# One PSUM tile per bank for Strassen's down products, and the attention's value projection placed ahead of the rotations

## The chip, the core and the metric

The kernel runs on one core of a Trainium2 chip. Its metric is the device time of one execution in microseconds (us). It is stated as the median of several executions; the profile is a further execution of the same program, recorded by the hardware profiler.

TensorE (PE in the profile, its weight loads PEld) does the matrix products into PSUM, an accumulation memory of eight banks. VectorE (DVE), ScalarE (ACT) and GpSimd (POOL) read PSUM or SBUF and do the elementwise work; SP here only issues DMAs.

## The reference

One step of a two-layer streaming encoder for 512 prompt tokens and 64 tokens of a running stream, 576 in all, at width 1024. Cut to what matters:

```python
for i in range(2):
    h = rmsnorm(x, norm_mix[i])
    y = pool_mixer(h) if i == 0 else attn_mixer(h)
    x = x + y
    u = relu(rmsnorm(x, norm_mlp[i]) @ w_up[i])       # 1024 -> 4096
    x = x + (u * u) @ w_down[i]                       # 4096 -> 1024
y = rmsnorm(x, norm_final)

# attn_mixer: p = h @ w_in is cut into q (16 heads of 64), k and v (4 heads), qi (8 index heads),
# ki (1 index key) and wi (8 weights); q, k, qi, ki are rotated by position
score = sum_h relu(qi_h . ki / 8) * wi_h              # masked by chunk
idx = top_k(score)                                    # up to 256 keys for each query
o = softmax(q . k[idx] / 8) @ v[idx];  y = o @ w_o
```

Keys, values and index keys of the step are outputs as well.

## The kernel before, in words

All matrices lie transposed: features on the 128 partitions, the 576 tokens along the free axis, in two halves of 288 (`HT`). Each fp32 operand is split into a high and a low part, so that one product takes three matmuls (high by high, high by low, low by high). A block of weights, 128 output columns of a matrix, is loaded as one tile by a DMA on ACT's queue, cast by ACT (L166: `wh`) and completed by a subtraction on DVE (L167: `wl`). `jobs` lists these blocks in the order of their use; `next_unit` and `next_block` take from it and keep a few units ready ahead.

The program is written as if it ran in sequence. A scheduler (`schedule_with_timeline_sim`, L1214) then decides the order of the instructions on each engine; only the pool mixer and the tail `last()` have parts ordered by hand. Each engine runs its queue in the built order.

The stages follow each other at L1126 to L1133: the pool mixer, the first MLP, the attention, the second MLP with the tail.

**MLP.** `split_x` scales and splits the residual into `xs` and adds up its squares on the way (L251, L252). Eight up blocks (`project`, L226, 48 matmuls each) make one c, a quarter of the hidden width. The norm's statistics come behind the first ups: `stats` sums the squares over partitions on PE (`st`, L284), a chain of small DVE operations makes the reciprocal root, `spread` puts it on all partitions by two matmuls with a diagonal (`rb`, L264) and ACT copies it to SBUF (L265). Only then can `activated` evacuate an up tile (DVE, L327, the tile times `rb`, cut at zero; ACT squares it). So the up tiles made before that stay in PSUM.

The down product of a c is done by Strassen's scheme (in the first MLP for all four c, in the second for three): `factors` (L335) makes seven right factors from the activations; the weights' sums are made on POOL. `Pair` (L359) handles two output blocks with three accumulators a, b and c. `opening` (L368) runs three products of 12 matmuls, `opened` (L376) lets DVE, and at the last c POOL, read them; `closing` (L391) runs four more products into a, b, c and b, each read by one DVE addition (L396). `down` (L398) goes over four pairs.

**PSUM.** Two pools serve the whole kernel: `ps`, three tiles of two banks, and `po`, two tiles of one bank (L54, L55, handed out by `psum`, L91, and `psum1`, L94). In a `Pair` a and b are the halves of one `ps` tile and c is a `po` tile. The ups take `ps` tiles, `st` and `rb` take `po` tiles. A tile of a pool with n buffers waits for the readers of the n-th tile before it.

**Attention.** `ki` and the first index query block `pj` are projected (48 matmuls each), then the norm is spread, the tables cs and sn are multiplied by it, and `ki` is rotated (L782 to L785). `rope` projects two blocks and rotates them; the two index query halves go first (on DVE, L814 to L827), through DRAM, and come back by the loads into `qis`. Behind them stands the value projection (L1077 to L1095): two blocks `w_v` of 264 columns, the tokens in five groups in the order 1, 2, 3, 4, 0; each has 24 matmuls into half a `ps` tile, one ACT copy to `V` and one DVE operation for `wi`. Into its last group four index scores are mixed. Then come the key rotation, four query rotations, and the units of attention: `scores`, `softmax` (DVE L910, ACT L911), `transpose` (PE L952, `pt`), `values`. `pace` mixes index scores (`ix`, L864 and L879; read by ACT L872 or L874; added up on DVE L882 and L884) into these rotations' projections. `top_k(i)` runs 16 or 18 rounds of a maximum (L895) and a replacement (L896) on DVE and makes the mask (L899); its place in the program is ahead of the first scores of query block i.

The second MLP's first up follows the output projection `wo`, whose tiles DVE adds to the residual (L1123).

Of the kernel before, what the change touches and what calls it, by code (L numbers as in the profile page):

```python
# [24 lines left out]
NIDX = 8  # L25
# [18 lines left out]
def pool_dsa_kernel(ctx: ExitStack, tc: tile.TileContext, a, o):  # L44
    nc = tc.nc
    act, dve, pool, pe = nc.scalar, nc.vector, nc.gpsimd, nc.tensor
# [4 lines left out]
    raws = ctx.enter_context(tc.tile_pool(name="raws", bufs=2))  # L51
    norms = ctx.enter_context(tc.tile_pool(name="norms", bufs=1))
    tiny = ctx.enter_context(tc.tile_pool(name="tiny", bufs=4))
    ps = ctx.enter_context(tc.tile_pool(name="ps", bufs=3, space=PSUM))  # L54
    po = ctx.enter_context(tc.tile_pool(name="po", bufs=2, space=PSUM))  # L55
    dram = ctx.enter_context(tc.tile_pool(name="dram", bufs=1, space=bass.MemoryType.DRAM))

    count = [0]
# [1 line left out]
    def uid(s):  # L60
        count[0] += 1
        return f"{s}_{count[0]}"

    phase = {}

    @contextmanager
    def stage(**pools):

        with ExitStack() as st:
            phase.clear()  # L70
            for name, bufs in pools.items():
                phase[name] = st.enter_context(tc.tile_pool(name=uid(name), bufs=bufs, reuse_waits="tile"))
            yield

    def slot(tag, s, dt=F32R):
# [4 lines left out]
    def pair_slot(tag, s, dt=F32R, n=T):  # L80
        return slot(tag, s, dt)[:, :2 * n].rearrange("p (h t) -> p h t", h=2)
# [6 lines left out]
    def small(n, s):  # L88
        return tiny.tile([P, n], F32, tag=s, name=uid(s))

    def psum(s="ps"):  # L91
        return ps.tile([P, 2, 512], F32, tag="ps", name=uid(s))

    def psum1(s="po"):  # L94
        return po.tile([P, 512], F32, tag="po", name=uid(s))

    def f32(t):
        return t.bitcast(F32)
# [4 lines left out]
    def const(shape, name, dt=F32, pool=None):  # L103
        return (pool or cst).tile(shape, dt, tag=name, bufs=1, name=name)
# [35 lines left out]

    mlp_jobs(0, 4)
    jobs.extend(("block", a["w_in"][j], KT * P) for j in range(5))
    jobs.extend(("block", a["w_v"][j], 4 * 264) for j in range(2))
    jobs.extend(("block", a["w_in"][j], KT * P) for j in range(5, 15))
    for _ in range(2):
        jobs.extend(("block", a["w_o"][m], KT * P) for m in range(KT))
    mlp_jobs(1, 3)
# [78 lines left out]
    def project(pt, w, xs, between=iter(()), cols=((0, HT), (HT, HT))):  # L226

        n = len(xs)
        for k in range(n):
            next(between, None)  # L230
            wh, wl = at(w, k)
            for i, (wt, part) in enumerate(((wh, 0), (wh, 1), (wl, 0))):
                for h, (c, m) in enumerate(cols):
                    pe.matmul(  # L234
                        pt[:, h, :m], wt, xs[k][:, part, c:c + m],
                        start=(k == 0 and i == 0), stop=(k == n - 1 and i == 2),
                    )

    class Norm:
# [14 lines left out]
        def stats(self):  # L254
            pt = psum1("st")
            token_sums(pt, self.s2)
            self.r = rms(pt)

        def spread(self):
            diag = diagonals(self.r)  # L260
            self.rb = tmp("rb" + self.s, "rb", 1)
            for h in range(2):
                pb = psum1("rb")
                pe.matmul(pb[:, :HT], ones, diag[:, h * HT:(h + 1) * HT], start=True, stop=True)  # L264
                act.copy(self.rb[:, h * HT:(h + 1) * HT], pb[:, :HT])  # L265
            return self.rb
# [44 lines left out]
    def split_x(gi, norm, tags, add=dve):  # L311
        xs = []
        for k in range(KT):
            t = pair_slot(tags[k], "xs")
            split(t, x[k], gv[:, gi, k:k + 1])
            norm.add(k, add if k < 6 else dve)
            xs.append(t)
        return xs

    def mlp(layer, gi, strassen, add=dve, end=None):  # L320
        norm = Norm(f"m{layer}")
        xs = split_x(gi, norm, ["xs"] * KT, add)
# [36 lines left out]
        class Pair:  # L359


            def __init__(self, c, q, us):
                self.c, self.q, self.us = c, q, us
                ab = psum("ab")
                self.a, self.b, self.c_ = ab[:, 0], ab[:, 1], psum1("c")
                self.lo, self.hi = ([x[2 * q + i][:, c0:c0 + HT] for i in range(2)] for c0 in (HT, 0))

            def opening(self, parts=((0, 1, 2, 3),)):  # L368
# [36 lines left out]
        v = None  # L405
# [350 lines left out]
    def attention():  # L756
        nonlocal x
        norm = Norm("a")
        xs = split_x(2, norm, ["xs"] * KT)
# [7 lines left out]
        V = const([P, 9, 256], "V", pool=cst)  # L767
        wi = const([P, 5, 8], "wi", pool=cst)
# [6 lines left out]
        r = norm.r  # L775
        p0 = psum("pj")
        project(p0, next_block(), xs)
        rb = norm.spread()
        pool.tensor_tensor(cs, cs, rb, ALU.mult)
        dve.tensor_tensor(sn, sn, rb, ALU.mult)  # L780
        t1, t2, ki = tmp("t1"), tmp("t2"), tmp("ki")
# [281 lines left out]

        def pace():

            due = 0
            for k in range(10 * KT):
                while due <= k and done[0] < 3 * NIDX:
                    next(index)
                    due += PACE[min(done[0] // NIDX, 2)]  # L1070
                    done[0] += 1
                yield

        done = [0]
        index = (None for i in range(1, 5) for _ in index_scores(i))

        wv = [next_block(), next_block()]  # L1077
        for i in (1, 2, 3, 4, 0):
            n = P if i < 4 else TS
            pt = psum("v")[:, 0]  # L1080
            for k in range(KT):
                if i == 0 and k % 2:
                    next(index, None)
                    done[0] += 1
                wh, wl = wv[k // 4][k % 4 // 2]
                sl = slice((k % 2) * 264, (k % 2 + 1) * 264)
                for j, (part, wt) in enumerate(((0, wh), (1, wh), (0, wl))):
                    pe.matmul(pt[:n, :264], xs[k][:, part, i * P:i * P + n], wt[:, sl],  # L1088
                              start=(k == 0 and j == 0), stop=(k == KT - 1 and j == 2))
            vi = i if i < 4 else 8  # L1090
            act.activation(V[:n, vi], pt[:n, :256], AF.Copy, scale=r[:n, i:i + 1])
            dve.tensor_scalar(wi[:n, i], pt[:n, 256:264], r[:n, i:i + 1], NIDX ** -0.5, ALU.mult, ALU.mult)
        act.activation(small(8, "e1"), wi[:, 0], AF.Exp)
        nc.sync.dma_start(o["v_p"], V[:, 0:4])
        nc.sync.dma_start(o["v_s"], V[:TS, 8])  # L1095

        between = pace()
        qd, ks = {}, []
        (k1, k2), st = rope(False)
        nc.sync.dma_start(o["k"][0], k1)  # L1100
        nc.sync.dma_start(o["k"][1], k2)
        for g in range(NKV):
            t = pair_slot("x", "k")
# [16 lines left out]
        for m in range(KT):  # L1120
            pt = psum("wo")
# [1 line left out]
            dve.tensor_tensor(x[m][:, 2 * P:], x[m][:, 2 * P:], pt[:, 0, :T - 2 * P], ALU.add)  # L1123
# [106 lines left out]
```

## Time and profile before

| | |
|---|---|
| three executions | 1164.63, 1165.96, 1166.82 us |
| median | 1165.96 us |
| profiled execution, its own time | 1169.65 us |
| span of its instructions | 1167.8 us |
| instructions | 20621 |
| PE busy | 95% of the span |
| DVE busy | 70% |
| ACT busy | 45% |
| POOL busy | 30% |
| granted PE clock, mean | 0.98 |
| DMA moved | 116.68 MB |

The profiled execution's time is 1.85 us longer than its span, and 3.69 us above the median of the three. Times in the trace are counted from the start of the span. In a row of the timeline the first two numbers are start and length, both in us; "xN" joins N instructions of one kind; in brackets stands how long the engine sat idle just before, and which instruction released it. In a row of waits the numbers are the sum in us, how many times, and the longest. In a row of a group stand the busy time, the mean length of one in ns, and the idle time ahead of it. A row of stretches gives the busy time of PE, PEld, DVE, ACT and POOL with the number of instructions, and then the granted clock of PE as a share of full speed.

### The profile page before, as it was taken

How to read it: one execution, taken by the hardware profiler on the slowest of the kernel's cores; microseconds unless marked ns; L12 is line 12 of the kernel's file. 1: busy time of each engine (PE TensorE's matmuls, PEld its weight loads, DVE VectorE, ACT ScalarE, POOL GpSimd, SP SyncE). 2: the span in 40 equal slices, each digit the busy share in tenths (PEclk: the TensorE clock that was granted, in tenths of full speed). 3: DMA queues.
4: the chain of work that ended last, by engine and by line, in shares of the span. 5: the costliest groups of instructions: out<-in, count | busy, mean ns of one | idle time of the engine just before them, and what ended most of it. 6: DMA issues, size and time to landing. Idle time of an engine off the chain costs nothing.

```text
span 1167.8 us, 20621 instructions
## 1 busy us (share of the span) xinstructions
PE 1110.5 (95%) x8244; PEld 1090.6 (93%) x8244; DVE 817.0 (70%) x1478; ACT 528.9 (45%) x968; POOL 349.9 (30%) x274
## 2 busy tenths in 40 slices
PE   7999999999999999798989999999999999989995
PEld 6999999999999999797979999999999989989995
DVE  7776666767667786759999853876766767775434
ACT  5644344335334444253368665654344335333331
POOL 7711410330240351117775341101410330350002
PEclk8999999999999999798989999999999999999998
DMA  5421241232232134366652432431241132114212
GB/s 172 114 75 52 73 145 55 75 125 73 73 108 91 38 113 161 101 197 158 170 154 74 121 104 81 157 109 55 73 145 55 57 125 90 55 55 122 77 37 82
DMA packets 51152, 116.68 MB, mean 100 GB/s; under 512 B 9345, under 2 KB 22960, under 8 KB 51056
## 3 DMA queue, kind: packets, MB, share of 16 engines
q10 hardware_dynamic: 23184, 84.45, 23.1%
q1 hardware_dynamic: 27872, 30.90, 9.2%
q8 instruction: 65, 1.06, 0.4%
q14 instruction: 31, 0.25, 0.1%
HBM read 99.73 MB, written 13.25 MB: 97 GB/s over the span
## 4 chain that ended last, share of the span: by engine, by line
PE 60%; DVE 15%; issue 12%; POOL 5%; DMA 4%; ACT 3%; SPq 0%; DVEq 0%; ACTq 0%; POOLq 0%
PE up L234 30%; PE ab L356 8%; DVE wl L167 5%; PE dn L234 4%; PE pj L234 4%; PE c L356 3%; DVE work L896 2%; PE o L971 2%; DMA raw<-in_w_up 2%; PE wa L234 1%; DMA pair<-in_w_down 1%; DVE m L895 1%; POOL sum L194 1%; PE v L1088 1%; PE pb L720 1%
## 5 line engine op out<-in xcount | busy, mean ns | idle before, releaser
L234 PE MATMUL up<-xs,wh 128*128 128x288 f32 x2048 | 355.9, 295 | 1.5 <-DVE v L327 1.3
L234 PEld LDWEIGHTS up<-xs,wh 128*128 128x128 f32 x2048 | 299.8, 188 | 2.5 <-DVE v L327 1.7
L356 PE MATMUL ab<-u,wh 128*128 128x288 f32 x1120 | 227.2, 297 | 11.4 <-DVE x L396 5.8
L166 ACT CAST wh<-raw 128x512 fp32r<-128x512 f32 (+1 forms) x210 | 126.0, 619 | 206.2 <-DMA raw<-in_w_up 61.9
L234 PE MATMUL up<-xs,wl 128*128 128x288 f32 x1024 | 219.4, 295 | 0.0
L167 DVE TENSOR_TENSOR wl<-raw,wh 128x512 fp32r<-128x512 f32 (+1 forms) x186 | 144.3, 784 | 70.7 <-ACT wh L166 68.9
L356 PEld LDWEIGHTS ab<-u,wh 128*128 128x128 f32 x1120 | 179.4, 189 | 15.3 <-DVE x L396 8.6
L356 PE MATMUL ab<-u,wl 128*128 128x288 f32 x560 | 165.5, 298 | 2.0 <-DVE wl L167 1.9
L234 PEld LDWEIGHTS up<-xs,wl 128*128 128x128 f32 x1024 | 164.2, 188 | 0.0
L167 DVE TENSOR_TENSOR wl<-pair,wh 128x512 fp32r<-128x512 f32 x112 | 101.4, 917 | 30.5 <-ACT wh L166 30.0
L194 POOL TENSOR_TENSOR sum<-sum,pair 128x512 f32<-128x512 f32 x28 | 41.2, 1472 | 265.4 <-DVE wl L167 265.4
L186 POOL TENSOR_TENSOR sum<-pair 128x512 f32<-128x512 f32 x28 | 38.0, 1357 | 266.7 <-DMA pair<-in_w_down 266.7
L166 ACT CAST wh<-sum 128x512 fp32r<-128x512 f32 x84 | 51.0, 621 | 145.8 <-POOL sum L187 47.7
L356 PEld LDWEIGHTS ab<-u,wl 128*128 128x128 f32 x560 | 105.4, 189 | 3.9 <-DVE wl L167 3.5
L166 ACT CAST wh<-pair 128x512 fp32r<-128x512 f32 x112 | 68.2, 620 | 86.4 <-PE up L234 40.7
L356 PE MATMUL c<-u,wh 128*128 128x288 f32 x448 | 92.5, 295 | 0.4 <-ACT wh L166 0.4
L167 DVE TENSOR_TENSOR wl<-sum,wh 128x512 fp32r<-128x512 f32 x84 | 71.2, 858 | 26.2 <-ACT wh L166 25.4
L327 DVE SCALAR_TENSOR_TENSOR v<-up,rbm 128x576 f32<-128x576 f32 x64 | 48.2, 755 | 58.6 <-PE up L234 57.2
L234 PE MATMUL pj<-xs,wh 128*128 128x288 f32 x448 | 83.5, 304 | 4.1 <-DVE t L783 4.1
L234 PEld LDWEIGHTS pj<-xs,wh 128*128 128x128 f32 x448 | 70.1, 197 | 5.8 <-DVE t L783 4.9
L356 PEld LDWEIGHTS c<-u,wh 128*128 128x128 f32 x448 | 72.4, 189 | 0.7 <-ACT wh L166 0.7
L356 PE MATMUL c<-u,wl 128*128 128x288 f32 x224 | 66.0, 296 | 0.0
(224 smaller groups left out, 1974.6 us busy)
## 6 DMA issues: line engine op xcount, KB each, us to landing
raw<-in_w_up ACTq DMA_DIRECT2D x64, 512.0 KB, 3.6
pair<-in_w_down ACTq DMA_DIRECT2D x56, 512.0 KB, 3.6
raw<-in_w_o ACTq DMA_DIRECT2D x16, 512.0 KB, 4.1
raw<-in_w_in ACTq DMA_DIRECT2D x15, 512.0 KB, 4.0
q<-st SPq DMA_DIRECT2D x32, 144.0 KB, 2.6
q<-q SPq DMA_DIRECT2D x16, 256.0 KB, 3.0
raw<-in_w_down ACTq DMA_DIRECT2D x8, 512.0 KB, 3.5
x<-in_x SPq DMA_DIRECT2D x8, 288.0 KB, 6.3
```

The lines of the kernel that those rows point to most:

```text
L166: act.copy(h, src)
L167: how["sub"].tensor_tensor(l, src, f32(h), ALU.subtract)
L186: pool.tensor_tensor(s1, a21, a22, ALU.add)
L194: pool.tensor_tensor(s2, s2, a12, ALU.add)
L234: pe.matmul(pt[:, h, :m], wt, xs[k][:, part, c:c + m], start=(k == 0 and i == 0), stop=(k == n - 1 and i == 2),)
L327: dve.scalar_tensor_tensor(v, pt[:, :, :HT], 0.0, halves(norm.rb), ALU.max, ALU.mult)
L356: pe.matmul(bank[:, :HT], wt, ut, start=first and j == 0 and i == 0, stop=last and j == 3 and i == 2, skip_group_check=True)
L720: pe.matmul(pt[:, c0:c0 + rhs.shape[1]], lhs, rhs, start=n == 0, stop=n == len(steps) - 1)
L895: dve.max(m8[:np_], wk[:np_])
L896: dve.match_replace(wk[:np_], m8[:np_], wk[:np_], TAKEN)
L971: pe.matmul(oc[:, 2 * s + hh], pT[:, c:c + P], V[:, kt, vs], start=kt == 0, stop=kt == i)
L1088: pe.matmul(pt[:n, :264], xs[k][:, part, i * P:i * P + n], wt[:, sl], start=(k == 0 and j == 0), stop=(k == KT - 1 and j == 2))
```

## The change

The pools `ps` and `po` are no longer made once for the whole kernel but anew in each of the four stages. The pool mixer and the attention get three tiles of two banks and two of one bank as before; both MLPs get **two** tiles of two banks and **four** of one bank. The pools wait for a reuse tile by tile (`reuse_waits="tile"`, which the other stage pools had already). A `Pair` takes three tiles of one bank.

In the attention the value projection goes to just behind `norm.spread()`, ahead of the multiplication of cs and sn. Its groups now come in the order 0 to 4, without index scores among them, and into one-bank `po` tiles. Its two output DMAs move with it, and so stand on SP ahead of the index queries' stores and loads. In `jobs` the two `w_v` blocks come behind two `w_in` blocks instead of five. `pace` begins with index scores after `KT` = 8 steps instead of at once.

```diff
-    ps = ctx.enter_context(tc.tile_pool(name="ps", bufs=3, space=PSUM))
-    po = ctx.enter_context(tc.tile_pool(name="po", bufs=2, space=PSUM))
...
             for name, bufs in pools.items():
-                phase[name] = st.enter_context(tc.tile_pool(name=uid(name), bufs=bufs, reuse_waits="tile"))
+                space = {"space": PSUM} if name in ("ps", "po") else {}
+                phase[name] = st.enter_context(tc.tile_pool(name=uid(name), bufs=bufs, reuse_waits="tile", **space))
...
-    jobs.extend(("block", a["w_in"][j], KT * P) for j in range(5))
+    jobs.extend(("block", a["w_in"][j], KT * P) for j in range(2))
     jobs.extend(("block", a["w_v"][j], 4 * 264) for j in range(2))
-    jobs.extend(("block", a["w_in"][j], KT * P) for j in range(5, 15))
+    jobs.extend(("block", a["w_in"][j], KT * P) for j in range(2, 15))
...
-                ab = psum("ab")
-                self.a, self.b, self.c_ = ab[:, 0], ab[:, 1], psum1("c")
+                self.a, self.b, self.c_ = (psum1(t) for t in "abc")
...
         rb = norm.spread()
+
+        wv = [next_block(), next_block()]
+        for i in range(5):
+            n = P if i < 4 else TS
+            pt = psum1("v")
+            for k in range(KT):
...
+                    pe.matmul(pt[:n, :264], xs[k][:, part, i * P:i * P + n], wt[:, sl],
+                              start=(k == 0 and j == 0), stop=(k == KT - 1 and j == 2))
+            vi = i if i < 4 else 8
+            act.activation(V[:n, vi], pt[:n, :256], AF.Copy, scale=r[:n, i:i + 1])
+            dve.tensor_scalar(wi[:n, i], pt[:n, 256:264], r[:n, i:i + 1], NIDX ** -0.5, ALU.mult, ALU.mult)
+        nc.sync.dma_start(o["v_p"], V[:, 0:4])
+        nc.sync.dma_start(o["v_s"], V[:TS, 8])
         pool.tensor_tensor(cs, cs, rb, ALU.mult)
...
         def pace():
 
-            due = 0
+            due = KT
...
-        wv = [next_block(), next_block()]
-        for i in (1, 2, 3, 4, 0):
-            n = P if i < 4 else TS
-            pt = psum("v")[:, 0]
-            for k in range(KT):
-                if i == 0 and k % 2:
-                    next(index, None)
-                    done[0] += 1
...
         act.activation(small(8, "e1"), wi[:, 0], AF.Exp)
-        nc.sync.dma_start(o["v_p"], V[:, 0:4])
-        nc.sync.dma_start(o["v_s"], V[:TS, 8])
...
-    with stage(slots=1, xs=1, tmps=6):
+    with stage(slots=1, xs=1, tmps=6, ps=3, po=2):
         pool_mixer()
-    with stage(u=1, xs=1, acts=1, tmps=3, pairs=1, more=2):
+    with stage(u=1, xs=1, acts=1, tmps=3, pairs=1, more=2, ps=2, po=4):
         mlp(0, 1, 4, pool)
-    with stage(slots=1, xs=1, cst2=1, tmps=6):
+    with stage(slots=1, xs=1, cst2=1, tmps=6, ps=3, po=2):
         attention()
-    with stage(xs=1, u=1, acts=1, tmps=3, pairs=1, more=2):
+    with stage(xs=1, u=1, acts=1, tmps=3, pairs=1, more=2, ps=2, po=4):
         mlp(1, 3, 3, end=last)
```

More of the change, by code (lines that the diff above doesn't have):

```diff
@@ L91, in psum @@
     def psum(s="ps"):
-        return ps.tile([P, 2, 512], F32, tag="ps", name=uid(s))
+        return phase["ps"].tile([P, 2, 512], F32, tag="ps", name=uid(s))
     def psum1(s="po"):
-        return po.tile([P, 512], F32, tag="po", name=uid(s))
+        return phase["po"].tile([P, 512], F32, tag="po", name=uid(s))
     def f32(t):
@@ L778, in attention @@
         rb = norm.spread()
+        wv = [next_block(), next_block()]
[3 more added lines that the diff above has]
+            for k in range(KT):
+                wh, wl = wv[k // 4][k % 4 // 2]
+                sl = slice((k % 2) * 264, (k % 2 + 1) * 264)
+                for j, (part, wt) in enumerate(((0, wh), (1, wh), (0, wl))):
+                    pe.matmul(pt[:n, :264], xs[k][:, part, i * P:i * P + n], wt[:, sl],
[5 more added lines that the diff above has]
+        nc.sync.dma_start(o["v_s"], V[:TS, 8])
         pool.tensor_tensor(cs, cs, rb, ALU.mult)
@@ L1075, in attention @@
         index = (None for i in range(1, 5) for _ in index_scores(i))
-        wv = [next_block(), next_block()]
-        for i in (1, 2, 3, 4, 0):
-            n = P if i < 4 else TS
-            pt = psum("v")[:, 0]
-            for k in range(KT):
-                if i == 0 and k % 2:
-                    next(index, None)
-                    done[0] += 1
[L1085 to L1092, printed above, removed]
         act.activation(small(8, "e1"), wi[:, 0], AF.Exp)
-        nc.sync.dma_start(o["v_p"], V[:, 0:4])
-        nc.sync.dma_start(o["v_s"], V[:TS, 8])
         between = pace()
```

## The prediction, made before the changed kernel ran

> **What bounds the kernel now.** I read the page's busy times and slices first, then PE's waits, then the timeline where a wait is long or where the change acts, and last the stretches with their clock.
>
> ```profile
> PE 1110.5 (95%) x8244; PEld 1090.6 (93%) x8244; DVE 817.0 (70%) x1478; ACT 528.9 (45%) x968; POOL 349.9 (30%) x274
> ...
> PE   7999999999999999798989999999999999989995
> ...
> PEclk8999999999999999798989999999999999999998
> ...
> L356 PE MATMUL ab<-u,wh 128*128 128x288 f32 x1120 | 227.2, 297 | 11.4 <-DVE x L396 5.8
> ```
>
> PE is the bound: 1110.5 of 1167.8 us, and no slice but those about the attention's start, and the first and the last, is clearly below 9 tenths. The change adds no matmul, so it can win only from the 57.3 us in which PE is idle and from stretches at a low clock. Its waits say whose the idle time is:
>
> ```profile
> PE ab L356 <- DVE x L396: 5.8, 11, 1.3
> PE pt L952 <- ACT p L911: 5.2, 2, 5.1
> PE ix L864 <- ACT rl L872: 5.2, 1, 5.2
> PE pj L234 <- DVE t L783: 4.1, 1, 4.1
> ...
> PE ab L356 <- ACT wh L166: 2.9, 2, 1.5
> ```
>
> The first row is the stall that the product banks are about: 11 times the products waited for DVE to read an accumulator. The fourth is the one that the moved values could fill. The second and third stand further on in the attention; DVE is behind both, as shown below.
>
> **Starts of the MLPs: two up tiles instead of three.** Here the change adds a wait. Before, three ups run before `rb` exists; with `ps` at two, the third up's first matmul waits for DVE's L327 of the first up, and so for the whole norm chain.
>
> ```profile
> 48.39 0.77 PE L234 MATMUL up<-xs,wh 128*128 128x288 f32 x4
> ...
> 61.80 0.76 DVE L252 TENSOR_TENSOR s<-s,sq 128x576 f32<-128x576 f32 x1 [1.32 <-POOL s L252]
> ...
> 63.08 0.75 DVE L252 TENSOR_TENSOR s<-s,sq 128x576 f32<-128x576 f32 x1
> ...
> 65.84 1.16 PE L284 MATMUL st<-ones,s 128*128 128x2 f32 x10
> ...
> 69.17 1.24 PE L264 MATMUL rb<-diag,ones 128*128 128x288 f32 x4 [0.25 <-DVE diag L274]
> ...
> 71.69 0.79 PE L234 MATMUL up<-xs,wh 128*128 128x288 f32 x4 [1.29 <-DVE v L327]
> ```
>
> The order of before puts 131 up matmuls between 48.39 and `st` at 65.84: 0.133 us each, 6.3 us for an up of 48. In the first MLP after, PE's order is up, up, st, rb, rb, up. The two ups end at about 62; `st` needs the last sum of squares. The POOL sum ends at 61.80, and the two DVE additions now stand back to back: 61.8 + 0.76 + 0.75 = 63.3. From `st` to `rb` I take 69.17 - 65.84 = 3.33, and from `rb` to the next up that waits for L327 71.69 - 69.17 = 2.52. The third up starts at 63.3 + 3.33 + 2.52 = 69.2 and ends at 75.4; before, three ups were done at 71.69: **+3.7 us**. (The first up now also waits for the pool mixer's last evacuation, about 1 us; that is inside the wait for 63.3 and costs nothing.) PE runs in order, so the other five ups of this c and all products queue behind the waiting one, and DVE's and ACT's work on them with it; nothing later gives the time back, since PE is the bound.
>
> ```profile
> 750.82 0.70 PE L234 MATMUL up<-xs,wh 128*128 128x288 f32 x4
> ...
> 753.82 0.48 DVE L1123 TENSOR_TENSOR x<-x,wo 128x320 f32<-128x320 f32 x1
> ...
> 758.68 1.15 PE L284 MATMUL st<-ones,s 128*128 128x2 f32 x10
> ...
> 765.80 1.21 PE L264 MATMUL rb<-diag,ones 128*128 128x288 f32 x4 [0.52 <-DVE diag L274]
> ...
> 766.64 0.90 PE L234 MATMUL up<-xs,wh 128*128 128x288 f32 x4
> ...
> 767.48 1.42 DVE L327 SCALAR_TENSOR_TENSOR v<-up,rbm 128x576 f32<-128x576 f32 x2 [0.46 <-ACT rbm L265]
> ```
>
> In the second MLP the stage's new pool makes the first up wait for the last L1123, which ends at 753.82 + 0.48 = 754.3, where before PE went on at 750.82: 3.5 us idle. Then up, st, up: 754.3 + 6.3 + 1.15 + 6.3 = 768.1, `rb`, and the third up again waits for the first L327: `rb` to its end was 767.48 + 0.7 - 765.80 = 2.4, so 770.5 instead of 766.64: **+3.9 us**. Bounds of each: nothing (if the chain is as quick as PE) and 6.3 (one whole up without cover).
>
> To that comes the clock:
>
> ```profile
> 401.00:405.00 4.00, 3.35 (x14) 3.35 (x15) 3.73 (x6) 2.84 (x5) 1.12 (x1) 0.58 0.01 2
> 468.00:478.00 10.00, 3.70 (x15) 2.48 (x15) 4.12 (x12) 1.20 (x4) 1.97 (x1) 0.59 0.18 55
> ...
> 548.00:555.00 7.00, 5.29 (x20) 5.01 (x20) 7.00 (x16) 3.43 (x7) 1.51 (x2) 0.53 0.62 154
> ```
>
> After a break PE comes back at about half clock: 0.42 of 4 us, 1.7 us, in the first row; 0.47 of 7 us, 3.3 us, in the last. The new breaks, some 4.5 of 7 us idle at the first start and 3.5 us in one piece at the second, resemble these rows. I take the middle, 2.6 us each, **+5.2** for both, with bounds of 0 and 3.3 each. The Trainium skill's page "TensorE: Matmul & The Clock Gate", in "HAM oscillation — how this bites in real kernels", asks only that no idle gap exceed about 3.4 us; by that the first start, whose pieces are 1 to 2 us, would keep its clock, and the sum would be 2.6 us lower. The trace speaks against it: its first row stands behind a gap of about 2 us.
>
> **Down stages: four single banks.** Seven stages of four pairs. DVE's reads of a, b and c now release three tiles separately, and the next pair opens in whatever bank came free; the order of after puts about 24 matmuls, 3.2 us, between a read and the product that needs its bank, against waits of at most 1.3 us. The whole gain to be had is the row of 5.8 us. Some reads stay queued behind a weight subtraction on DVE, so I take 60%: **-3.5 us**. Bounds: -5.8, and +5.8 if single banks wait as often again, since c now shares its four banks with a and b.
>
> **Entry to the attention.** Before, 57 matmuls of `ki` and `pj` lay among the last products; after, all products come first and then three projections, 19 us of cover while the residual's splits and squares run. The work is the same; what can go is part of the wait before `st`.
>
> ```profile
> 468.01 1.26 PE L284 MATMUL st<-ones,s 128*128 128x2 f32 x10 [2.28 <-DVE s L252]
> 471.45 2.29 PE L264 MATMUL rb<-diag,ones 128*128 128x288 f32 x4 [2.17 <-DVE diag L274]
> 477.84 1.33 PE L234 MATMUL pj<-xs,wh 128*128 128x288 f32 x4 [4.11 <-DVE t L783]
> ```
>
> The 2.28 us go, the 2.17 us stay: **-2.5 us** with a little from the products. Bounds -5 (these two with part of the last c's waits) and +4 (the projections no longer fill the products' waits, up to the fourth row's size).
>
> **The moved values.** What moves is 120 matmuls, five ACT copies, five small DVE operations and two DMAs; nothing is added. The values' groups now start right behind `rb` and fill the 4.11 us. The two output DMAs go ahead of the index queries' on SP, but `V` is ready about 15 us behind `rb` and those loads were due 21 us behind it: no cost; without that cover, the issue of two DMAs. `pace` and the five groups put the first index score about 3 us later behind `rb`; four more weight subtractions are done by then on DVE, which evens it out. So PE gains 4 to 7 us here, but what comes next is DVE:
>
> ```profile
> 516.00:550.00 34.00, 28.82 (x205) 28.13 (x204) 33.15 (x68) 13.47 (x28) 23.25 (x14) 0.98 0.55 141
> 550.00:594.00 44.00, 38.93 (x272) 38.32 (x271) 43.17 (x92) 16.64 (x32) 31.67 (x21) 0.93 0.59 163
> 594.00:640.00 46.00, 44.77 (x346) 42.42 (x346) 42.96 (x166) 40.15 (x133) 28.73 (x23) 0.94 0.41 109
> 640.00:740.00 100.00, 99.31 (x786) 95.74 (x786) 64.75 (x168) 60.67 (x142) 33.49 (x29) 1.00 0.36 109
> ```
>
> DVE is busy 33.15 of 34 and 43.17 of 44 us: from 516 to 594 it sets the pace, PE's two 5 us waits lie there, and PE wins only if DVE's order changes. It does:
>
> ```profile
> L895 DVE MAX8 m<-work 128x8 f32<-128x256 f32 (+2 forms) x40 | 20.9, 528 | 0.6
> L896 DVE MATCH_REPLACE8 work<-m,work 128x256 f32<-128x256 f32 (+2 forms) x39 | 19.9, 510 | 0.0
> ```
>
> ```profile
> 584.95 0.92 DVE L899 TENSOR_SCALAR work<-work 128x384 f32<-128x384 f32 x1
> ...
> 588.42 0.69 DVE L895 MAX8 m<-work 128x8 f32<-128x512 f32 x1
> ...
> 589.94 0.69 DVE L895 MAX8 m<-work 128x8 f32<-128x512 f32 x1
> ...
> 592.86 0.28 DVE L910 CUSTOM_DVE_ANT_0 p<-sc,mask 128x128 f32<-128x128 f32 x1
> ```
>
> In DVE's order after, the first softmax (592.86 here) has 15 fewer operations ahead of it: five rounds of top_k(3) at 589.94 - 588.42 = 1.52, two of top_k(2) at 0.528 + 0.510 = 1.04, one L899 of 0.92: 7.6 + 2.1 + 0.9 = 10.6 us. These rounds aren't saved, they come later between the units of attention, where the third row still has DVE at 42.96 of 46 us. By the order, about 7 to 8 us are still owed when DVE gets slack (64.75 of 100 us from 640 on). So I take **-7.5 us**. Bounds: -10.6, and +3 (all rounds paid back, index scores 3 us later).
>
> **Sum.** 3.7 + 3.9 + 5.2 - 3.5 - 2.5 - 7.5 = -0.7 us. The tail and the pool mixer keep their order and count as nothing; PE covers what is left there. 1169.65 - 0.7 = 1168.95 us as a profiled execution; that one stood 3.69 us over the median, so 1165.3 us.
>
> **Rivals.**
>
> *DVE takes the attention's gain back* (slower). The deferred rounds fall due before the masks of blocks 2 and 3, and DVE has only 3 of 46 us free there; if it stays above 95% busy until about 640, softmax is as late as before and -7.5 becomes 0: 1165.3 + 7.5 = 1172.8. For it: the third row; against it: PE's wait of 5.1 us on the first softmax would still move.
>
> *Starts at full clock, gains whole* (faster). The half clock doesn't strike (-5.2), the banks take all of 5.8 (-2.3) and the attention all of 10.6 (-3.1): 1165.3 - 10.6 = 1154.7. For it: full clock before through a 1.29 us gap at 71.69; against it: the row at 401.
>
> *The banks don't do what they are for.* The waits on DVE are really waits on weights, as the row of 2.9 us with ACT's cast hints, and only change their name: -3.5 becomes 0, 1168.8.
>
> *Single banks put the down stages at half clock* (slower). The accumulator waits become more frequent, and one row like that at 401 in each of seven stages costs 7 x 1.7 = 12 us: 1177. The slices show full clock through all down stages with their 11 waits, which speaks against it. The same page's "A second HAM failure mode: psum-queue depth-cycling" reports such an oscillation where results cycle through banks; no run here shows it.
>
> **How the numbers follow.** Below 0.2%, 2.3 us, a measurement of this kernel can't be told from no change. Forecast 0.35, with its own range of 1160 to 1171: faster 0.12, same 0.15, slower 0.08. DVE takes it back: 0.30, slower. Full gains: 0.22, faster. Banks without effect: 0.08, same 0.02, slower 0.06. Half clock in the down stages: 0.05, slower. Together faster 0.34, same 0.17, slower 0.49: the likeliest single case is no change, with more ways to lose than to win. The range goes from 1154.5, the full gains, to 1177, the unknown costs' ends without their sums.
>
> **What the profile after would show.** Right: a PE wait of 3.5 us on L1123 at the second MLP's start and about 4.5 us about `st`, `rb` and the third up at the first; the granted clock under 0.7 there; "ab" or a, b, c waits on L396 under 2.5 us in all; no wait on L783; the first `pt` some 10 us earlier behind `rb`. Wrong: waits on L396 as large as before, or PE idle on softmax between 594 and 640 by several us more; or a second MLP that starts without a wait.

## The result, and the profile after

The changed kernel took 1181.59 us (median of 4 executions, 1176.38 to 1183.02), the kernel before 1166.39 (median of 4): a ratio of 1.0116, 95% interval 1.0073 to 1.0158. It is slower, by some 15 us, outside the predicted range; the forecast was no change. The profiled execution has a span of 1181.3 us against 1167.8, 13.5 us more.

The page of the changed kernel:

```profile
PE 1117.8 (95%) x8244; PEld 1096.1 (93%) x8244; DVE 811.7 (69%) x1478; ACT 529.9 (45%) x968; POOL 354.4 (30%) x274
...
PE   7989989999999999999979999899999999999995
...
PEclk8989999999999999999989999999999999999998
...
L356 PE MATMUL b<-u,wh 128*128 128x288 f32 x672 | 139.1, 300 | 10.2 <-DVE x L395 8.1
```

The instructions of PE are as many as before. PE's idle time grew from 57.3 to 63.5 us, and its busy time by 7.3 with the same instructions, so matmuls ran longer: a new dip stands in the third slice of both rows, at the first MLP's start. The last line is the surprise: the single bank b alone waits 8.1 us for the residual's additions, more than a and b together did before. PE's waits:

```profile
PE b L356 <- DVE x L395: 8.1, 8, 2.2
PE pt L967 <- ACT p L926: 7.8, 4, 6.5
...
PE up L234 <- DVE x L1118: 3.4, 1, 3.4
...
PE up L234 <- DVE v L327: 2.7, 2, 1.4
PE ix L879 <- ACT rl L887: 2.7, 1, 2.7
PE c L356 <- DVE x L395: 2.4, 3, 1.2
...
PE ix L879 <- DMA qi<-qi: 1.7, 1, 1.7
```

(L395 and L1118 are the lines 396 and 1123 of before; in the runs below the same additions stand at L394 to L397 and L1118 to L1121.) To place the 13.5 us, I took from each trace the start of the same PE instructions: the first up of each later c, the last `wo` matmul and the first `dn`, a matmul of the down products of the second MLP's last c, which are not by Strassen's scheme. Each column below is how much longer (+) or shorter than in before a stretch was, in us, from those starts; the first stretch starts with the span. PE takes the first up of the next c ahead of a c's down products, so the second row ends ahead of those of c = 2.

| stretch, by its end | before's end | after | banks only | values only | pools per stage | t3 first | subtractions on POOL |
|---|---|---|---|---|---|---|---|
| first MLP, first eight ups | 103.54 | +7.3 | +6.2 | 0.0 | +0.2 | +4.8 | +5.7 |
| its down stages of c = 0 and 1, with the next ups | 297.76 (first up of c = 3) | +7.7 | +6.4 | +0.2 | -0.1 | -0.7 | +1.3 |
| its down stages of c = 2 and 3, and the attention | 750.68 (last wo) | -5.3 | -0.2 | -5.6 | -6.3 | -4.7 | -3.2 |
| second MLP, first eight ups | 804.98 | +5.6 | +5.7 | +0.6 | +2.1 | +5.4 | +5.6 |
| its Strassen stages | 1101.34 (first dn) | -2.4 | -2.8 | -0.2 | 0.0 | -2.2 | -4.6 |
| tail | 1167.8 | +0.6 | +0.5 | +0.5 | +0.4 | +0.5 | +0.6 |

The five kernels on the right are the experiments below. One execution scatters by some 3 us, as the runs of before show (1164.6 to 1171.3), so a difference of 1 us in this table isn't to be read. "The first MLP's down stages" means the second row below.

The third row adds up three things. Two more cuts, at the first product of c = 3 (394.41 in before) and at the end of the spread `rb` (473.73), split it into the stage of c = 2, the stage of c = 3 with the entry to the attention, and the attention from the spread on: +1.1, -1.2 and -5.3 in the changed kernel, +2.0, +0.5 and -2.7 with the banks only, 0.0, -1.6 and -4.0 with the values only.

**The starts.** PE's timeline and its stretches at the first MLP:

```profile
62.99 1.16 PE L284 MATMUL st<-ones,s 128*128 128x2 f32 x10
66.31 2.29 PE L264 MATMUL rb<-diag,ones 128*128 128x288 f32 x4 [2.17 <-DVE diag L274]
69.97 1.30 PE L234 MATMUL up<-xs,wh 128*128 128x288 f32 x4 [1.37 <-DVE v L327]
```

```profile
64.00:72.00 8.00, 4.46 (x14) 3.29 (x14) 4.58 (x15) 3.31 (x7) 0.00 (x0) 0.61 0.19 66
72.00:80.00 8.00, 8.00 (x48) 8.00 (x48) 4.15 (x7) 2.55 (x4) 0.00 (x0) 0.75 0.00 0
```

The third up starts at 69.97 (forecast 69.2) and runs with the clock granted at 0.61 and then 0.75 of full speed: 0.25 of the second stretch is 2 us, and some of the first. The norm chain is the predicted one, st to rb 3.3 us, rb to up 3.7 instead of 2.5, and `rb` itself takes 2.29 us instead of 1.24. At the second MLP:

```profile
763.45 0.48 DVE L1118 TENSOR_TENSOR x<-x,wo 128x320 f32<-128x320 f32 x1
764.08 0.76 PE L234 MATMUL up<-xs,wh 128*128 128x288 f32 x4 [3.40 <-DVE x L1118]
...
782.09 0.77 PE L234 MATMUL up<-xs,wh 128*128 128x288 f32 x4 [1.37 <-DVE v L327]
```

Its 3.40 us on the last L1118 is the wait that was forecast as 3.5, and the third up waits for L327 as forecast. The stretch behind the first wait has its clock at 0.79, so 0.21 of 8 us, 1.7 us, where 2.6 was forecast:

```profile
764.00:772.00 8.00, 7.92 (x48) 7.95 (x49) 4.59 (x7) 3.54 (x6) 0.00 (x0) 0.79 0.47 140
```

**The down stages.** This is the end of the first stage, DVE's and ACT's rows with the product that waits, in the changed kernel:

```profile
162.23 0.33 ACTq L125 DMA_DIRECT2D raw<-in_w_up  x1
...
165.02 1.14 ACT L166 CAST wh<-raw 128x512 fp32r<-128x512 f32 x2 [3.72 <-DMA raw<-in_w_up]
...
165.67 1.44 DVE L167 TENSOR_TENSOR wl<-raw,wh 128x512 fp32r<-128x512 f32 x1 [3.10 <-ACT wh L166]
167.03 0.44 DVE L395 TENSOR_TENSOR x<-x,b 128x288 f32<-128x288 f32 x1
...
167.53 0.54 PE L356 MATMUL b<-u,wh 128*128 128x288 f32 x2 [1.82 <-DVE x L395]
```

The read of b (167.03) stands in DVE's queue behind a weight subtraction (165.67), which waited 3.10 us for a cast, which waited 3.72 us for a load. The product t3 had left bank b on PE long before; t4 waits 1.82 us for the read. The end of the second stage repeats it: the subtraction at 266.63 waited 3.13 us for its cast, the cast 3.75 us for its load, and t4 at 268.85 waits 2.20 us for b's read. In the table's second row the products' waits for these additions grew from 1.5 us in before to 6.4 us. The same place in before:

```profile
153.40 0.46 DVE L396 TENSOR_TENSOR x<-x,ab 128x288 f32<-128x288 f32 x1 [0.82 <-PE ab L356]
...
154.22 0.62 ACT L166 CAST wh<-raw 128x512 fp32r<-128x512 f32 x1 [2.81 <-DMA raw<-in_w_up]
...
154.88 1.27 DVE L167 TENSOR_TENSOR wl<-raw,wh 128x512 fp32r<-128x512 f32 x1 [1.02 <-ACT wh L166]
156.07 0.44 DVE L396 TENSOR_TENSOR x<-x,c 128x288 f32<-128x288 f32 x1
```

The load is just as late there (2.81 us of waiting for it), but the read of b (153.40) stands ahead of the subtraction. So my theory after the comparison was: **D**, the scheduler put DVE's reads of the last pair behind the next weights' subtractions, and these wait for a load. Its rival: **A1**, the single banks left too little PE work between t3 and t4, which both go into b (one product of 12 matmuls, 1.6 us), wherever the subtractions stand.

### The profile page after: what moved, and what is told of

It is laid out like the page before. It is cut to its first block, busy times and chain, and to the rows that moved or that the text cites. A ratio compares the mean times of both kernels' runs of the same rounds, so it can differ in the third digit from the quotient of the medians.

```text
span 1181.3 us, 20612 instructions
## 1 busy us (share of the span) xinstructions
PE 1117.8 (95%) x8244; PEld 1096.1 (93%) x8244; DVE 811.7 (69%) x1478; ACT 529.9 (45%) x968; POOL 354.4 (30%) x274
## 4 chain that ended last, share of the span: by engine, by line
PE 59%; issue 14%; DVE 14%; POOL 6%; DMA 4%; ACT 3%; SPq 0%; DVEq 0%; ACTq 0%; POOLq 0%
PE up L234 33%; DVE wl L167 6%; PE dn L234 4%; PE b L356 3%; PE o L986 3%; DMA raw<-in_w_up 2%; PE wo L234 2%; PE a L356 2%; PE wa L234 2%; PE c L356 2%; PE sc L947 2%; PE pt L967 1%; POOL sum L194 1%; POOL sum L186 1%; POOL sum L187 1%
## 5 line engine op out<-in xcount | busy, mean ns | idle before, releaser
L234 PE MATMUL up<-xs,wh 128*128 128x288 f32 x2048 | 360.4, 298 | 7.3 <-DVE x L1118 3.4
L234 PEld LDWEIGHTS up<-xs,wh 128*128 128x128 f32 x2048 | 304.6, 191 | 8.8 <-ACT sq L251 4.8
L167 DVE TENSOR_TENSOR wl<-raw,wh 128x512 fp32r<-128x512 f32 (+1 forms) x186 | 139.6, 756 | 95.2 <-ACT wh L166 93.5
L356 PE MATMUL b<-u,wh 128*128 128x288 f32 x672 | 139.1, 300 | 10.2 <-DVE x L395 8.1
L356 PEld LDWEIGHTS b<-u,wh 128*128 128x128 f32 x672 | 108.1, 190 | 14.3 <-DVE x L395 10.4
L356 PE MATMUL b<-u,wl 128*128 128x288 f32 x336 | 99.6, 299 | 2.4 <-DVE wl L167 2.3
L327 DVE SCALAR_TENSOR_TENSOR v<-up,rbm 128x576 f32<-128x576 f32 x64 | 48.2, 756 | 73.1 <-PE up L234 70.1
L356 PE MATMUL a<-u,wh 128*128 128x288 f32 x448 | 92.2, 297 | 2.6 <-DVE u L347 2.0
L234 PE MATMUL pj<-xs,wh 128*128 128x288 f32 x448 | 80.2, 296 | 0.0
L356 PEld LDWEIGHTS a<-u,wh 128*128 128x128 f32 x448 | 72.4, 189 | 3.4 <-DVE u L347 2.3
L234 PEld LDWEIGHTS pj<-xs,wh 128*128 128x128 f32 x448 | 67.3, 190 | 0.7
```

The source lines that it names most:

```text
L167: how["sub"].tensor_tensor(l, src, f32(h), ALU.subtract)
L234: pe.matmul(pt[:, h, :m], wt, xs[k][:, part, c:c + m], start=(k == 0 and i == 0), stop=(k == n - 1 and i == 2),)
L327: dve.scalar_tensor_tensor(v, pt[:, :, :HT], 0.0, halves(norm.rb), ALU.max, ALU.mult)
L356: pe.matmul(bank[:, :HT], wt, ut, start=first and j == 0 and i == 0, stop=last and j == 3 and i == 2, skip_group_check=True)
```

## The experiments

The kernel before ran beside each group: medians 1167.97, 1167.27 and 1168.07 us for runs 1 to 4, 5 to 8 and 9 to 10.

**1. The PSUM part alone.** The pools per stage, the counts and the three single tiles as in the change; the values and `jobs` as before.

```diff
-                ab = psum("ab")
-                self.a, self.b, self.c_ = ab[:, 0], ab[:, 1], psum1("c")
+                self.a, self.b, self.c_ = (psum1(t) for t in "abc")
...
+    with stage(u=1, xs=1, acts=1, tmps=3, pairs=1, more=2, ps=2, po=4):
...
```

> The PSUM part alone: pools per stage, two up tiles and four single banks in the MLPs, a Pair of three single tiles; the values stay behind the index queries. From the two profiles the MLPs lose 7.3 + 5.6 us at their starts and 10.7 - 2.4 us in their down stages, 21 us, and the attention gains 8 us. Theory A (the two parts are independent: the MLPs' loss is the PSUM part's, the attention's gain is the moved values'): about 21 us over before, 1187 us. Rival B (the attention's gain comes from the pools of its own, not from the moved values): about 13 us over before, 1179 us.

Measured: 1186.48 us, ratio 1.0165 (1.0146 to 1.0183).

```profile
PE b L355 <- DVE x L394: 8.8, 8, 2.3
...
PE pj L233 <- DVE t L781: 4.1, 1, 4.1
PE up L233 <- DVE x L1121: 3.6, 1, 3.6
```

The loss of 18.5 us is the PSUM part's, with the same three waits as after; the wait of `pj` on the rotation, 4.1 us, is there as in before. The table's third row gains nothing (-0.2), though as a sum of +2.5 ahead of the attention's spread and -2.7 behind it; what the -2.7 comes from stays open, as DVE does 37 rounds of top_k ahead of the first softmax here as in before. Theory A gave the time (1187), rival B's 1179 falls. The expectation's 10.7 and 8 us were read at other places of the traces; at the cuts used here they are 8.8 (the stages of c = 0 to 2) and 6.5 (the rest of the third row).

**2. The values alone.** The changed kernel with before's two pools, counts and Pair.

```diff
+    ps = ctx.enter_context(tc.tile_pool(name="ps", bufs=3, space=PSUM))
+    po = ctx.enter_context(tc.tile_pool(name="po", bufs=2, space=PSUM))
...
-                self.a, self.b, self.c_ = (psum1(t) for t in "abc")
+                ab = psum("ab")
+                self.a, self.b, self.c_ = ab[:, 0], ab[:, 1], psum1("c")
...
```

> The moved values alone, with before's two pools for the whole kernel and before's Pair. Theory A: the MLPs as before and the attention 8 us shorter, about 1158 us; the wait on L1118 at the second MLP's start is gone. Rival B: no gain, 1166 us.

Measured: 1162.76 us, ratio 0.9955 (0.9938 to 0.9972), 5 us faster, less than the 8 expected; the MLPs are as before to 0.6 us in each stretch. With run 1 this adds up to the change: 1.0165 x 0.9955 = 1.0119, against 1.0116.

```profile
PE pt L969 <- ACT p L928: 8.9, 6, 6.9
PE ab L357 <- DVE x L397: 5.5, 9, 1.3
PE ix L881 <- ACT rl L889: 3.1, 1, 3.1
```

PE's wait on the rotation is gone, but its wait on the softmax is longer, 6.9 us in one piece.

**3. The pools per stage, with before's tiles.** The changed kernel with three and two tiles in the MLPs and before's Pair.

```diff
-                self.a, self.b, self.c_ = (psum1(t) for t in "abc")
+                ab = psum("ab")
+                self.a, self.b, self.c_ = ab[:, 0], ab[:, 1], psum1("c")
...
-    with stage(u=1, xs=1, acts=1, tmps=3, pairs=1, more=2, ps=2, po=4):
+    with stage(u=1, xs=1, acts=1, tmps=3, pairs=1, more=2, ps=3, po=2):
...
```

> The changed kernel with three two-bank tiles and two single ones in the MLPs too, and before's Pair, so that of the PSUM part only the pools per stage are left. Theory A (the third up tile is what the starts lose, and the down stages lose by the new tiles): the first MLP's start as before, the wait of 3.4 us on L1118 stays, so 3 to 5 us over the kernel with the values alone. Rival C (the pools per stage are what shifts the schedule of the down stages): the waits on the residual's reads stay near 10 us and the time near the changed kernel's, over 1172 us.

Measured: 1167.13 us, ratio 0.9998 (0.9982 to 1.0013).

```profile
PE ab L356 <- DVE x L396: 7.2, 11, 1.4
...
PE up L234 <- DVE x L1119: 3.1, 1, 3.1
```

Against run 2 it is 4.4 us slower by the medians, as theory A expected; the two traces differ by only 0.9 us (1164.2 against 1163.3), so most of the 4.4 can't be placed. With the third up tile back, the first MLP's start and the down stages are as before (+0.2 and -0.1 in the table), and of the second start 2.1 us of the 5.6 stay, with the wait on L1119. So the third up tile is worth about 7 us at the first start and 3.5 at the second. Rival C gave a time over 1172, and falls, although the waits on L396 are 7.2 here.

**4. t3 ahead of b21.** The changed kernel with the first two closing products, and their weights, exchanged.

```diff
-                for bank, factor, out, b2 in ((self.a, "b21", self.lo[0], 0), (self.b, "t3", self.hi[1], 0),
+                for bank, factor, out, b2 in ((self.b, "t3", self.hi[1], 0), (self.a, "b21", self.lo[0], 0),
...
-            yield split_unit(a12)
             yield split_unit(a21)
+            yield split_unit(a12)
```

> The changed kernel with the first two closing products exchanged (t3 ahead of b21, and their weight units too), so that two products instead of one stand between t3 and t4, which both go into bank b. Theory A1 (b waits because of the true order write, read, write with too little work between): the 8.1 us of b on DVE's L395 fall below 3, and the time by 5 us or more. Rival D (DVE's read is queued behind weight subtractions that wait for a late cast and a late load, so that it is late wherever the product stands): the waits stay at 6 us or more, and the time within 2 us of the changed kernel's.

Measured: 1173.84 us, ratio 1.0053 (1.0033 to 1.0073), 7.7 us under the changed kernel's median, and the first MLP's down stages went from +7.7 to -0.7.

```profile
PE b L356 <- DVE x L395: 3.7, 5, 1.4
```

The time is what A1 expected and the wait nearly so (less than 3), and D's expectation failed. But the exchange doesn't tell the two apart, since it also moves the reads in DVE's queue: in this run's trace the reads of b and a stand at 158.76 and 159.13, ahead of the late subtraction at 161.60, whose cast waited 3.77 us for its load. Run 6 tells them apart.

**5. The values alone, t3 first.** The exchange of run 4 on the kernel of run 2.

```diff
-                for bank, factor, out, b2 in ((self.a, "b21", self.lo[0], 0), (self.b, "t3", self.hi[1], 0),
+                for bank, factor, out, b2 in ((self.b, "t3", self.hi[1], 0), (self.a, "b21", self.lo[0], 0),
...
-            yield split_unit(a12)
             yield split_unit(a21)
+            yield split_unit(a12)
```

> The values alone with before's PSUM pools, and the closing products with t3 ahead of b21. In the changed kernel that exchange took 7.7 us. If it works by the room between t3 and t4 wherever the banks lie, the 5.5 us of waits of ab on L397 shrink to about 2 and the time goes to about 1159 us, below both kernels. If it only mends what the single banks did to the schedule, the time stays at the values-alone 1163 us.

Measured: 1160.84 us, ratio 0.9944 (0.9932 to 0.9956).

```profile
PE ab L357 <- DVE x L397: 6.3, 8, 1.4
```

The waits didn't shrink, and the interval overlaps that of run 2: with before's banks the exchange gives 1.9 us by the medians, not clear of the noise. So the room between t3 and t4 is not what it works by; that in run 4 it mended the schedule of the single banks fits this, but isn't shown by this run alone.

**6. The last pair's subtractions on GpSimd.** The changed kernel, products in their old order.

```diff
-                    product(bank, next_unit(), self.us, factor, js, False, True)
+                    product(bank, next_unit(sub=pool if self.q == 3 else dve), self.us, factor, js, False, True)
```

> The changed kernel; the weight subtractions that are issued during the last pair of a stage (those of the next c's second and third up) go to GpSimd instead of DVE, so that in DVE's order the reads of the last pair's banks no longer stand behind them. Theory D (the read of b is late because DVE waits in order for a weight whose load and cast are late): b's long waits at the stages' ends (1.8 and 2.2 us in the first MLP) go, b on L395 falls from 8.1 to 4 us or less, the time by 3 to 6 us. Theory A1 (only too little PE work between t3 and t4): these waits stay above 1 us each and the time within 2 us.

Measured: 1174.44 us, ratio 1.0054 (1.0040 to 1.0068), 7.1 us under the changed kernel's median.

```profile
PE b L356 <- DVE x L395: 2.9, 6, 1.3
PE b L356 <- DVE x L382: 2.6, 3, 1.2
PE c L356 <- DVE x L395: 2.5, 4, 1.1
```

DVE's order at the stage's end, in this run:

```profile
159.93 0.45 DVE L395 TENSOR_TENSOR x<-x,b 128x288 f32<-128x288 f32 x1 [1.12 <-PE b L356]
...
163.51 0.62 ACT L166 CAST wh<-raw 128x512 fp32r<-128x512 f32 x1 [3.47 <-DMA raw<-in_w_up]
164.17 2.51 DVE L167 TENSOR_TENSOR wl<-raw,wh 128x512 fp32r<-128x512 f32 x2 [3.78 <-ACT wh L166]
```

The load is as late as ever (3.47 us), but b is read at 159.93, as soon as PE is done with it, and t4 doesn't wait, although as little PE work as ever stands between t3 and t4. b's waits on L395 fell from 8.1 to 2.9. That is D; A1, by which the waits stay, falls. Not all of the waiting is gone: that of b on the additions of `opened` (L382) rose from 0.2 to 2.6, and the three rows together went from 10.7 to 8.0. In the table's second row the waits on DVE's additions went from 6.4 to 3.2 us, and its clock is 1.00 where the changed kernel had 0.84 from 165 to 176.

**7. The up tiles in other banks.** The changed kernel with `po` made ahead of `ps` in both MLPs.

```diff
...
-    with stage(xs=1, u=1, acts=1, tmps=3, pairs=1, more=2, ps=2, po=4):
+    with stage(xs=1, u=1, acts=1, tmps=3, pairs=1, more=2, po=4, ps=2):
```

> The changed kernel with the order of the two PSUM pools exchanged in both MLP stages, so that the up tiles lie in other banks of PSUM. If the wait of 3.4 us on the last L1118 at the second MLP's start is for the banks that the last output tiles hold, it shrinks or goes to an earlier L1118, and the start is up to 3 us shorter; if it is for the old pool as a whole, it stays.

Measured: 1179.82 us, ratio 1.0101 (1.0087 to 1.0115).

```profile
PE b L356 <- DVE x L395: 6.5, 7, 2.2
...
PE up L234 <- DVE x L1118: 0.8, 1, 0.8
```

The wait went from 3.4 to 0.8 us, and the second start from +5.6 to +1.9: it was for the banks of the last output tiles, not for the old pool as a whole. The first MLP's down stages still cost +4.4.

**8. Index scores due at once.** The values alone with `due = 0`.

```diff
-            due = KT
+            due = 0
```

> The values alone, with the index scores due at once instead of after 8 steps. In the kernel with the values alone the first top_k round comes 55.8 us behind the spread's end, in before 45.6, and DVE sits idle for 25 us in that time. If the later index scores are what limits the gain (DVE is the bound behind them), the first round comes some 5 us earlier and the attention is 2 to 5 us shorter, 1158 to 1161 us. If the first index scores wait for their queries' transfer or their products' place on PE in any case, nothing changes: 1163 us.

Measured: 1162.23 us, ratio 0.9949 (0.9933 to 0.9965), the same as run 2 within the intervals. The first index score is added on DVE 30.4 us behind the spread instead of 36.3, but the first top_k round comes at 54.8 us, as late as ever. The trace says why. A round needs the scores of all eight heads, and the last four need the second half of the index queries. Its stores and loads on SP, before and after:

```profile
498.97 4.02 SPq L840 DMA_DIRECT2D qi<-st  x8
505.47 1.48 SPq L850 DMA_DIRECT2D qi<-qi  x3
```

```profile
523.44 3.65 SPq L855 DMA_DIRECT2D qi<-st  x8
532.30 1.48 SPq L865 DMA_DIRECT2D qi<-qi  x3
```

The value groups now stand ahead of the projections that make this half, so its stores start 34.8 us behind the spread instead of 25.2, and its loads 43.6 instead of 31.7; PE's wait of 1.7 us of `ix` on the load of `qi` in the changed kernel is the wait for it. In run 8 the loads start at 42.6 and the last four heads' matmuls at 45.6, however early the first four are. No run moves this half alone, so the cause is read from the order and the times, not isolated.

**9. Values, t3 first, scores at once.** Run 5 with the edit of run 8.

```diff
-            due = KT
+            due = 0
```

> The values alone with before's PSUM pools, t3 ahead of b21, and the index scores due at once: the three edits that each came out at 1160.8 to 1162.8 us. If their gains add up, 1159 to 1160 us; if the exchange and the earlier scores only shift the schedule, 1161 to 1163 us. Either way faster than before by more than its interval.

Measured: 1159.58 us, ratio 0.9927 (0.9911 to 0.9942), the fastest kernel here: 8.5 us under before, 22 under the changed kernel. That it beats run 2 alone is near the edge of the intervals.

**10. The changed kernel with the repairs of runs 4, 6 and 7.**

```diff
...
-                for bank, factor, out, b2 in ((self.a, "b21", self.lo[0], 0), (self.b, "t3", self.hi[1], 0),
+                for bank, factor, out, b2 in ((self.b, "t3", self.hi[1], 0), (self.a, "b21", self.lo[0], 0),
...
-                    product(bank, next_unit(), self.us, factor, js, False, True)
+                    product(bank, next_unit(sub=pool if self.q == 3 else dve), self.us, factor, js, False, True)
...
-    with stage(xs=1, u=1, acts=1, tmps=3, pairs=1, more=2, ps=2, po=4):
+    with stage(xs=1, u=1, acts=1, tmps=3, pairs=1, more=2, po=4, ps=2):
```

> The changed kernel with all three repairs: the last pair's weight subtractions on GpSimd, t3 ahead of b21, and the up tiles in the other banks. If the late reads of the last pair were the whole loss of the down stages, what is left against before is the first start (about 6 us), the second start without its long wait (about 2), less the single banks' gain in the second MLP (2 to 5) and the values' gain (5): 1163 to 1168 us. If the repairs of the reads each only mended part by chance, it stays above 1170 us.

Measured: 1178.48 us, ratio 1.0085 (1.0062 to 1.0109): the expectation failed, and the repairs don't add. The first MLP's down stages are mended (+0.1, by the same reckoning as in the table), but the second MLP's, -2.4 in the change, became +2.3. The timeline there:

```profile
864.76 0.62 ACT L166 CAST wh<-raw 128x512 fp32r<-128x512 f32 x1 [3.55 <-DMA raw<-in_w_up]
...
865.41 1.29 DVE L167 TENSOR_TENSOR wl<-raw,wh 128x512 fp32r<-128x512 f32 x1 [5.57 <-ACT wh L166]
...
866.62 0.44 DVE L395 TENSOR_TENSOR x<-x,b 128x288 f32<-128x288 f32 x1
...
867.12 0.54 PE L356 MATMUL b<-u,wh 128*128 128x288 f32 x2 [2.92 <-DVE x L395]
```

It is D once more: the next subtraction that was left on DVE now stands ahead of b's read, and its load is late. The reads stand at another place among the subtractions in each of the orders shown here (before, after, and runs 4, 6 and 10).

## Why the prediction was wrong

The profiled executions differ by +13.5 us where the sum had -0.7. By its terms, in us: the starts +12.9 for +12.8, the down stages +6.4 (six of the seven) for -3.5, the entry with the seventh -1.2 for -2.5, the values -5.3 for -7.5, the tail +0.6 for nothing. So 9.9 of the 14.2 us are the down stages'. The prediction named no change as the likeliest single case, though its chances together gave slower 0.49 and no change 0.17; no case had this loss, and the range ended at 1177. By its own steps:

- **Starts: right.** Forecast +3.7 and +3.9 with 2.6 each for the clock, 12.8 together; measured 7.3 + 5.6 = 12.9. That the sum fits so well is in part luck: the first start cost 1.0 more than its 6.3 and the second 0.9 less than its 6.5. Run 3 shows that the third up tile is the cause of most of it, run 7 that the wait on L1118 is one for banks. The low clock came at the first start behind idle pieces of 2.17 and 1.37 us. The rule of the Trainium skill's page "TensorE: Matmul & The Clock Gate" ("HAM oscillation — how this bites in real kernels"), read as a bound of about 3.4 us on a single gap, would have left the clock full there; the trace (0.61 and 0.75) disagrees, and decides.
- **Down stages: wrong, and this is the step that failed.** Forecast -3.5, bounds -5.8 and +5.8. Measured +7.7 in the first MLP's stages of c = 0 and 1, +1.1 in that of c = 2 and -2.4 in the second MLP's three, 6.4 together, beyond the bad bound by less than a trace scatters. The working counted PE's matmuls between a bank's read and the product that needs it and took 3.2 us as cover. What it left out is what stands ahead of the read on DVE: a subtraction that waits up to 3.1 us for a cast and a load. The prediction even said that some reads stay queued behind a subtraction, but took for that only 40% off the gain, with no term for the subtraction's own wait. About 1.7 us of the 7.7 is, by my estimate, the clock behind such a wait: in the changed kernel's stretch from 165 to 176 us it was granted at 0.84.
- **Entry and values: right mechanism, too large.** Forecast -2.5 - 7.5 = -10; measured -1.2 (with the products of c = 3) and -5.3, and 5 us in run 2 alone. The wait on L783 is gone, and DVE's order did hold fewer rounds ahead of the first softmax, 30 instead of 37, the seven that were forecast: it came 113.5 us behind the spread instead of 119.1. That is 5.6 us, not 10.6. The main reason is the start: the first top_k round began at 54.9 us instead of 45.6, where I had counted on some 3 us later. That term looked at the first index score (36.6 instead of 32.4) and at `pace`, and left out that the moved groups push back the second half of the index queries, as run 8 shows. The two rows (counted from the trace's start; the spread ends at 473.7 before and 488.7 after):

```profile
519.30 0.43 DVE L895 MAX8 m<-work 128x8 f32<-128x256 f32 x1
```

```profile
543.62 0.43 DVE L910 MAX8 m<-work 128x8 f32<-128x256 f32 x1
```

- **The rivals.** "DVE takes the attention's gain back" was half true: half of the 10.6 was lost, but ahead of the first top_k round and not behind the softmax. "Half clock in the down stages" was true for one wait; against it the prediction set full clock through all down stages of before, but its own row of 401 us (0.58) stands in one, as the products of c = 3 start at 394.41. That the single banks lose by DVE's order was none of them. The nearest was the banks without effect: its reason, that waits on DVE are really waits on weights, is what the trace shows, but it ended without a loss.

Of the signs named ahead, the wait on the residual at the second start came (3.4), the one on L783 went, and the clock fell under 0.7 at the first start (0.61) but not at the second (0.79); the waits on L395, 8.1 and 2.4 us, were the sign of being wrong.

What stays open is why the scheduler put the reads behind the subtractions with single banks. The runs show that it did, and that each edit moves it, but nothing in a profile shows its reasons.

## What to carry to other kernels

The cover of an accumulator's read isn't the matmuls between it and the next use: look at what stands ahead of the read in the reading engine's queue, and what that in turn waits for. When a pool of PSUM tiles is cut to feed another, look for the places where its full depth bridges a wait, here the norm's chain at a stage's start; one up tile fewer in flight there cost some 10 us with the clock, more than all the stalls that the banks were to mend. And when two edits are independent, as these are, run each alone: one gave 5 us and the other lost 18.

## What the runs showed of the hardware

The granted clock fell at the first MLP's start to 0.61 and 0.75 over 16 us although no single idle piece was longer than 2.2 us; PE was busy 4.46 of 8 us in the first of these stretches and all 8 in the second. Behind the gap of 1.82 us in the first down stage it fell to 0.84, and behind the gap of 2.20 us in the second it stayed at 1.00:

```profile
165.00:176.00 11.00, 9.18 (x58) 8.94 (x57) 5.68 (x9) 3.62 (x6) 1.56 (x2) 0.84 0.35 113
266.00:278.00 12.00, 9.80 (x74) 9.57 (x74) 8.48 (x14) 5.45 (x9) 1.88 (x2) 1.00 0.38 113
```

So of two gaps of like length one cost clock and the other none. What decides it, the runs don't show.
